# First expert's rows picked by a matmul with a selection matrix, a pair of experts moved ahead of additions, and the last tile's scattered rows added on TensorE

## The chip, the cores and the metric

The kernel runs on one core of a Trainium2 chip. The metric is the device time of one execution in microseconds (us); the table below has the runs of the kernel before.

## What is computed

Two transformer blocks run over 512 tokens of 1,024 channels. The change touches only the end of the second one, a mixture of 32 experts. Each token picks one of four groups of experts by a router's logits and then two experts in the group:

```
def _hierarchical_moe(xt, w_rg, b_rg, w_re, b_re, w_gate, w_up, w_down):
    ...
    y = jnp.zeros_like(xt)
    for e in range(N_EXPERTS):
        he = jax.nn.silu(xt @ w_gate[e]) * (xt @ w_up[e])
        y = y + combine[:, e:e + 1] * (he @ w_down[e])
    return y
```

`xt` is the normed row h2 of a token, `combine` its weight for the expert (zero for all but two). The result is added to x, and a last RMS norm with the vector `final_norm` gives the output. All is float32. Each expert has 3 MB of weights: gate and up of 1024x256, down of 256x1024.

## The kernel before, in words

**Routing (second_out, route_tile).** The 512 tokens stand in `xk` as four tiles of 128. For each tile t the kernel makes x (matmuls `pfo`), the logits (`plg`), the one-hot choice of both experts (`both`), and by matmuls with triangles of ones the rank of each token within its expert (`prank`). Each tile then adds to `ppos`, a table of which token stands in which slot of which expert. `pcnt` (sort_experts, line 1648) adds `both` over the four tiles, which gives the tokens of each expert. The normed rows go to DRAM as `h2d`, written by ScalarE with the channels regrouped (line 1509: it reads every eighth channel). The order in which the tiles take their steps on TensorE is written by hand in `SO`; the parts after `yield` in `tile` and `route_tile` are one step each, and the last entry of SO[1] is tile 3's last step, its two `ppos` matmuls.

**Tables.** `tables_of` turns `ppos` into token numbers (`tok`). The first three experts (AH = 3) are taken as they stand. The other 29 are sorted by their number of tokens: `cnt` (copied from `pcnt`), `key`, `rank`, and `order`, a chain on VectorE. SyncE reads `order` (line 1965) before it can issue the weight loads of any sorted expert, because it names the expert in DRAM.

**Experts (moe).** `gather(e)` fetches an expert's rows of h2d by an indirect DMA from GpSimd, `turn(e)` transposes them on TensorE and scales them by the norm's weights (`exT`), `gu(e)` multiplies by gate and up (`pgu`), `pair` or `scatter` by down. Experts with over 64 tokens scatter their rows to a buffer `yd` in DRAM; smaller ones go in pairs or fours: `ex_few` multiplies (`pyf`, float32), `ex_parts` scales the product on ScalarE and, as a remainder, on VectorE (`ys`), and `ex_add` brings the rows to their tokens by a matmul with a selection matrix (`psel`), after which VectorE adds PSUM to xk (line 1921). A selection is used for four tiles, two additions each; `waiting` holds the additions not yet done.

**Weights and PSUM.** Weight loads go through SyncE's queue in program order into rings of buffers: gate and up five experts ahead, down three ahead. Experts 0 to 2 and their weights are loaded before the routing ends. In this part `pb` hands out three PSUM banks in turn (tag A), `po` one (tag O); every fourth `psel` takes the one of `po`.

**End (finish).** Tiles 0 to 3 in turn: the scattered rows of tiles 2 and 3 are read back (`back`, two loads of 512 KB each into `yb`) and added by VectorE (`back_add`, line 2055), then the last four experts' rows are added. ScalarE squares each tile; one reciprocal root for all four (`rsq`, ten short VectorE instructions) and four scalings `fo` by VectorE (line 1941) follow, each with its output DMA. On TensorE the last part is in the order of the code (manual_schedule); elsewhere a scheduler places the instructions.

Of the kernel before, what the change touches and what calls it, by code (L numbers as in the profile page):

```python
# [24 lines left out]
NE = 32  # L25
# [5 lines left out]
PTC = 2  # L31
PS2 = (3, 2, 2)
FT = ((0, 4, 3),)
HB = 2


# [76 lines left out]
class K:  # L113
# [1344 lines left out]
    def second_out(self):  # L1458

        nc, I, sp = self.nc, self.I, self.sp  # L1460
        xk, yT, xp = self.xk, self.yT, self.xp
        self.ring.append(self.pool("experts1", side="right"))
        self.ep = self.pool("experts", side="right")
        rp = self.rp = self.pool("route", side="right")
        c = self.pool("out2")
        self.wsl = self.ep.tile([128, 32 + NX], F32, name="wsl")
        self.scat = self.ep.tile([128, 32 + NX], U32, name="scat")
        self.tok = self.ep.tile([128, 32 + NX], U32, name="tok")
        self.exinfo = self.ep.tile([1, 1 + NX], I32, name="exinfo")
        self.order = self.ep.tile([1, NE - AH], I32, name="order")  # L1470
        self.h2d = self.dr.tile([512, 1024], F32, name="h2d")
        wo = I["w_out_2"][0].rearrange("(k p) n -> p k n", p=128)
        us = [[self.wunit(wo[:, 4 + 2 * j:6 + 2 * j, c0:c0 + 512], [128, 2, 512]) for j in range(2)] for c0 in (0, 512)]
        wr, br = self.wr, self.br

        self.fwc = self.ep.tile([128, 8], F32, name="fwc")
        nc.gpsimd.dma_start(self.fwc, I["ffn_norm_2"][0].rearrange("(p k) -> p k", k=8))
        self.xgs = [rp.tile([128, 1024], F32, name="xg0")]
        nc.gpsimd.memset(self.xgs[0], 0.0)
        R = self.R = self.route_setup(rp)  # L1480

        def tile(t):

            x = xk[:, t, :]
            ss = sp.tile([128, 2], F32, name="h2s", bufs=2)
            for i, c0 in enumerate((0, 512)):
                p = self.pt("pfo") if i else self.pc("pfo")
                for k in range(4):
                    self.mm3(p, [y[:, 4 + k, t * 128:(t + 1) * 128] for y in yT], [x[:, k % 2, :] for x in us[i][k // 2]],
                             k == 0, k == 3)  # L1490
                o = xk[:, t, c0:c0 + 512]
                nc.vector.scalar_tensor_tensor(o, p, self.rsh[1][:, t:t + 1], o, op0=OP.mult, op1=OP.add)
                junk = self.op.tile([128, 512], F32, name="oT", tag="oT", bufs=2)
                nc.scalar.activation(junk, o, AF.Square, accum_out=ss[:, i:i + 1])
                yield
            rs = sp.tile([128, 1], F32, name="h2r", bufs=2)
            h = c.tile([128, 1024], F32, name="h2", tag="h2", bufs=2)
            y = c.tile([128, 8, 128], F32, name="x2T", tag="x2T", bufs=2)
            nc.vector.tensor_tensor(ss[:, 0:1], ss[:, 0:1], ss[:, 1:2], op=OP.add)
            self.turn8(y, x)  # L1500
            self.rsq(rs, ss[:, 0:1], 1.0 / D, EPS)
            yield
            pl = self.pt("plg")[:, :36]
            for k in range(8):
                nc.tensor.matmul(pl, y[:, k, :], wr[:, k, :], start=(k == 0), stop=(k == 7))
            nc.vector.scalar_tensor_tensor(R["lg"][:, t], pl, rs, br, op0=OP.mult, op1=OP.add)

            h3 = h.rearrange("p (k c) -> p k c", k=8)
            nc.scalar.activation(h3, x.rearrange("p (c k) -> p k c", k=8), AF.Copy, scale=rs)
            nc.scalar.dma_start(self.h2d[t * 128:(t + 1) * 128, :], h)  # L1510
            yield from self.route_tile(t, R, rp)

        tiles = [tile(t) for t in range(4)]
        for t in SO[0]:
            next(tiles[t], None)
        with self.tc.manual_schedule(engines={mybir.EngineType.PE}):
            for t in SO[1]:
                next(tiles[t], None)
        self.route_end()
        c.release()  # L1520
        self.op.release()


    def route_setup(self, c):
        nc = self.nc
        V = nc.vector
        R = {}
        io = R["io"] = c.tile([128, 128], F32, name="io")
        nc.gpsimd.iota(io, pattern=[[1, 128]], base=0, channel_multiplier=0, allow_small_or_imprecise_dtypes=True)
        R["rev"] = c.tile([128, 32], F32, name="rev")  # L1530
        V.tensor_scalar(R["rev"], io[:, :32], -1.0, 32.0, op0=OP.mult, op1=OP.add)
        jp = c.tile([128, 128], F32, name="jp2")
        nc.gpsimd.iota(jp, pattern=[[1, 128]], base=0, channel_multiplier=-1, allow_small_or_imprecise_dtypes=True)
        R["before"] = c.tile([128, 128], F32R, name="before")
        V.tensor_scalar(R["before"], jp, 0.0, None, op0=OP.is_gt)
        R["one"] = c.tile([128, 128], F32R, name="one2")
        V.tensor_scalar(R["one"], jp, -1000.0, None, op0=OP.is_ge)
        R["val"] = c.tile([128, 4, 2], F32, name="val")
        nc.gpsimd.iota(R["val"], pattern=[[128, 4], [512, 2]], base=-2048, channel_multiplier=1,
                       allow_small_or_imprecise_dtypes=True)  # L1540
        R["oh"] = c.tile([128, 4, 2, 32], F32, name="roh")
        R["both"] = c.tile([128, 4, 32], F32R, name="both")
        R["lg"] = c.tile([128, 4, 36], F32, name="lg")
        R["max"] = c.tile([128, 3, 4], F32, name="rmax")
        R["ps"] = c.tile([128, 4, 2], F32, name="rps")
        R["w"] = c.tile([128, 4, 2], F32, name="rw")
        R["pos"] = self.po("ppos")[:, :32]
        return R

    def route_tile(self, t, R, c):  # L1550
        nc = self.nc
        V = nc.vector
        rev = R["rev"]
# [22 lines left out]
        k, km = first(rest, m1, 32, "f1")  # L1576
        V.tensor_scalar(oh[:, 1], k, km, None, op0=OP.is_equal)
        V.tensor_tensor(both[:, t], oh[:, 0], oh[:, 1], op=OP.add)
        yield

        pr = self.pt("prank")[:, :64]
        for u in range(t):
            nc.tensor.matmul(pr[:, 0:32], R["one"], both[:, u], start=(u == 0), stop=False)
        nc.tensor.matmul(pr[:, 0:32], R["before"], both[:, t], start=(t == 0), stop=True)
        for k in range(2):
            x = new(32, "rx")
            V.tensor_tensor_reduce(x, pr[:, 0:32], oh[:, k], 1.0, 0.0, OP.mult, OP.add, R["ps"][:, t, k:k + 1])
# [322 lines left out]

        self.nc.vector.tensor_scalar(sel, self.io512, f, None, op0=OP.is_equal)

    def ex_add(self, sel, parts, n, t):

        for c in (slice(0, 512), slice(512, 1024)):
            self.nsel = getattr(self, "nsel", -1) + 1
            p = self.po("psel") if self.nsel % 4 == 3 else self.pb("psel")
            for k in range(2):
                self.nc.tensor.matmul(p, sel[:n, t * 128:(t + 1) * 128], parts[k][:n, c], start=(k == 0), stop=(k == 1))
            x = self.xk[:, t, c]  # L1920
            self.nc.vector.tensor_tensor(x, p, x, op=OP.add)

    def finish(self, add):

        nc = self.nc
        raw = self.eraw
        fs = raw("fs")[:, :8].rearrange("p (a t) -> p a t", a=2)
        os = []
        for t in range(4):
            add(t)  # L1930
            x = self.xk[:, t, :]
            o = raw("fo")
            nc.scalar.activation(o, x, AF.Square, accum_out=fs[:, 0, t:t + 1])
            os.append(o)
            for a, b, at in FT:
                if at != t:
                    continue
                self.rsq(fs[:, 1, a:b], fs[:, 0, a:b], 1.0 / D, EPS)
                for u in range(a, b):
                    o, rs = os[u], fs[:, 1, u:u + 1]  # L1940
                    nc.vector.scalar_tensor_tensor(o, self.xk[:, u, :], rs, self.fin, op0=OP.mult, op1=OP.mult)  # L1941
                    nc.sync.dma_start(self.out[0, u * 128:(u + 1) * 128, :], o)

    def moe(self):
# [37 lines left out]
            if e < NE:  # L1982
                X[e] = self.ex_turn(xgs[e % 2], mp, cap[e], e < 2)

        gather(0)
        gather(1)
        turn(0)
        gather(2)
        self.io512 = mp.tile([128, 512], F32, name="io512")
        nc.gpsimd.iota(self.io512, pattern=[[1, 512]], base=0, channel_multiplier=0, allow_small_or_imprecise_dtypes=True)  # L1990
# [79 lines left out]
        def step(e):  # L2070
# [22 lines left out]
            if full and e + 1 < NE:  # L2093
                waiting.extend(full + (t,) for t in range(4))

        for e in range(3):
            step(e)
        with tc.manual_schedule(engines={mybir.EngineType.PE}):
            for e in range(3, END):
                step(e)  # L2100
            load(END)
            for t in (2, 3):
                back(t)
            for e in range(END + 1, NE):
                gu(e)
                turn(e + 1)
                add(1)
                fold(e)
            add(4)
            pair(NE - 3)  # L2110
            full = pair(NE - 1)

        def last(t):
            if t > 1:
                back_add(t)
            self.ex_add(*full, t)

        self.finish(last)
        self.overflow(mp, xgs[0])
# [73 lines left out]
```

## Time and profile before

| | us |
|---|---|
| median of 3 runs | 1417.26 |
| lowest, highest | 1412.39, 1419.44 |
| profiled execution, time | 1414.1 |
| profiled execution, span | 1412.3 |
| TensorE busy | 1289.8 (91%) |
| VectorE busy | 939.0 (66%) |
| ScalarE busy | 611.6 (43%) |

The profile is of one execution; times in it count from the start of its span. The experts take about the last 300 us: from 1111 us on the 16 DMA engines move weights nearly without a pause until 1378 us, and the rest up to 1412.3 is the last additions, the norm and the output. Names such as `pgu` are the program's tiles. A float32 matmul shows as two records with two weight loads, so 64 records are 32 matmuls.

### The profile page before, as it was taken

Reading aid. Unit: us, or ns where it says so; the run is one execution under the profiler, and the core shown is the slowest. Engines: PE = TensorE matmul, PEld = TensorE weight load, DVE = VectorE, ACT = ScalarE, POOL = GpSimd, SP = SyncE. Lnnn points to the kernel's source line nnn. Section 1 sums busy time; section 2 is a strip of 40 time slices with the busy share of each in tenths; the row PEclk is TensorE's granted clock in tenths of the full one; section 3 lists DMA queues with packets and bytes.
Section 4 is the critical chain, followed back from the end, with each engine's and each line's share of the span. In section 5 each row is a group of like instructions: output and inputs, shape, how many; then the busy total and the mean of one; then the engine's idle time right before and its main releaser. Section 6 shows DMA issues by size and latency. Waiting matters only on the chain. (4 is left out here: it accounts for less than half of the span.)

```text
span 1412.3 us, 22313 instructions
## 1 busy us (share of the span) xinstructions
PE 1289.8 (91%) x7958; PEld 1021.3 (72%) x7958; DVE 939.0 (66%) x2062; ACT 611.6 (43%) x1197; POOL 312.4 (22%) x412
## 2 busy tenths in 40 slices
PE   4999999999989999899999999999999799998792
PEld 2888778877868788677877778787788776674350
DVE  5789998566643689998776463676766733534565
ACT  4553155445641474256574153777655211111122
POOL 5333032322220234133222020211110111111100
PEclk9999999999999999999998999999999799999996
DMA  9643355435132254416143356333333799999992
GB/s 342 161 129 108 102 147 159 132 99 182 60 135 61 91 127 150 139 46 166 39 124 109 140 173 172 96 82 128 97 127 118 255 389 387 369 373 375 391 401 91
DMA packets 166772, 246.18 MB, mean 174 GB/s; under 512 B 46788, under 2 KB 102810, under 8 KB 166660
## 3 DMA queue, kind: packets, MB, share of 16 engines
q1 hardware_dynamic: 161116, 234.95, 50.1%
q0 software_dynamic: 4864, 7.66, 2.0%
q10 hardware_dynamic: 680, 2.13, 0.4%
q8 instruction: 64, 1.05, 0.3%
q14 instruction: 48, 0.39, 0.1%
HBM read 220.69 MB, written 32.28 MB: 179 GB/s over the span
## 5 line engine op out<-in xcount | busy, mean ns | idle before, releaser
L185 DVE TENSOR_TENSOR wlo<-wraw,whi 128x1024 fp32r<-128x1024 f32 (+3 forms) x98 | 118.2, 1212 | 60.2 <-ACT whi L184 59.7
L184 ACT ACTIVATE whi<-wraw 128x1024 fp32r<-128x1024 f32 (+3 forms) x98 | 100.6, 1036 | 103.1 <-PE pout L223 42.9
L221 PE MATMUL pcm<-hTh,whi 128*128 128x256 f32 (+1 forms) x288 | 102.3, 355 | 9.2 <-DVE oa L531 4.3
L571 DVE SCALAR_TENSOR_TENSOR za<-zp,vec,za 128x783 f32<-128x783 f32 (+1 forms) x120 | 108.8, 914 | 0.5
L923 POOL TENSOR_SCALAR P<-P,ll 128x768 f32<-128x768 f32 (+1 forms) x80 | 73.7, 927 | 160.2 <-DVE ll L922 143.5
L223 PE MATMUL pcm<-hTh,wlo 128*128 128x256 f32 (+1 forms) x288 | 98.4, 342 | 0.1
L222 PE MATMUL pcm<-hTl,whi 128*128 128x256 f32 (+1 forms) x288 | 97.9, 340 | 0.0
L185 DVE TENSOR_TENSOR PTl<-pPT,PTh 128x512 fp32r<-128x512 f32 x104 | 70.3, 684 | 25.2 <-ACT PTh L184 24.7
L921 ACT ACTIVATE P<-pS,nm 128x768 f32<-128x768 f32 (+1 forms) x80 | 65.0, 816 | 36.6 <-DVE nm L919 30.4
L184 ACT ACTIVATE PTh<-pPT 128x512 fp32r<-128x512 f32 x104 | 60.7, 597 | 45.8 <-PE pPT L936 41.5
L1814 POOL DMA_INDIRECT xg<-h2d,tok x32 | 31.5, 986 | 214.2 <-PE pturn L1798 159.8
L1418 POOL TENSOR_SCALAR P<-P,l 128x384 f32<-128x384 f32 (+1 forms) x64 | 33.3, 536 | 184.6 <-DVE l L1417 167.5
L919 DVE TENSOR_REDUCE nm<-pS 128x1 f32<-128x768 f32 (+1 forms) x80 | 66.0, 843 | 9.6 <-PE pS L223 8.8
L221 PEld LDWEIGHTS pcm<-hTh,whi 128*128 128x128 f32 x288 | 54.8, 190 | 17.3 <-DVE oa L531 4.9
L221 PE MATMUL pcm<-hT0h,whi 128*128 128x512 f32 x144 | 59.5, 413 | 7.7 <-DVE oa L531 5.8
L936 PE MATMUL pPT<-ident,P 128*128 128x128 f32 x416 | 63.1, 280 | 1.0 <-DVE PTl L185 0.4
L968 POOL TENSOR_TENSOR oa<-oa,ot 64x256 f32<-64x256 f32 x40 | 37.4, 935 | 99.7 <-DVE ot L967 96.3
L223 PEld LDWEIGHTS pcm<-hTh,wlo 128*128 128x128 f32 x288 | 54.7, 190 | 6.5 <-DVE wlo L185 0.6
L222 PEld LDWEIGHTS pcm<-hTl,whi 128*128 128x128 f32 x288 | 54.9, 191 | 5.1 <-issue 0.5
L222 PE MATMUL pcm<-hT0l,whi 128*128 128x512 f32 x144 | 58.4, 406 | 0.0
L223 PE MATMUL pcm<-hT0h,wlo 128*128 128x512 f32 x144 | 58.4, 406 | 0.0
L221 PE MATMUL pS<-khi,qhi 96*128 96x256 f32 (+1 forms) x144 | 51.1, 355 | 4.3 <-ACT P L921 2.4
(521 smaller groups left out, 3633.0 us busy)
## 6 DMA issues: line engine op xcount, KB each, us to landing
wraw<-in_w_in_dram SPq DMA_DIRECT2D x56, 512.0 KB, 4.8
eraw<-in_w_expert_gate_dram SPq DMA_DIRECT2D x52, 512.0 KB, 10.8
eraw<-in_w_expert_up_dram SPq DMA_DIRECT2D x52, 512.0 KB, 11.3
wraw<-in_w_mod_dram SPq DMA_DIRECT2D x48, 512.0 KB, 6.0
wl<-in_w_expert_down_dram SPq DMA_DIRECT2D x32, 512.0 KB, 6.4
wh<-in_w_expert_down_dram SPq DMA_DIRECT2D x32, 512.0 KB, 10.8
wraw<-in_w_out_dram SPq DMA_DIRECT2D x24, 512.0 KB, 3.8
wraw<-in_w_expert_gate_dram SPq DMA_DIRECT2D x12, 512.0 KB, 13.5
```

What stands on the lines that cost most here:

```text
L184: nc.scalar.activation(hi, src, AF.Copy)
L185: return (eng or nc.vector).tensor_tensor(lo, src, hi.bitcast(F32), op=OP.subtract)
L221: mm(out, lhs[0], rhs[0], start=start, stop=False)
L222: mm(out, lhs[0], rhs[1], start=False, stop=False)
L223: mm(out, lhs[1], rhs[0], start=False, stop=stop)
L571: nc.vector.scalar_tensor_tensor(a[:, :nz], z[:, k:k + nz], cfw[:, i, k:k + 1], a[:, :nz], op0=OP.mult, op1=OP.add)
L919: nc.vector.tensor_reduce(nm, S, axis=AX.X, op=OP.max, negate=True)
L921: nc.scalar.activation(P, S, AF.Exp, bias=nm, accum_out=l)
L923: nc.gpsimd.tensor_scalar(P, P, l, 0.5, op0=OP.mult, op1=OP.mult)
L936: nc.tensor.transpose(p[:, jj, i * 128:(i + 1) * 128], Ps[i][:, (j + jj) * 128:(j + jj + 1) * 128], self.ident)
L968: nc.gpsimd.tensor_tensor(o, o, t, op=OP.mult)
L1418: nc.gpsimd.tensor_scalar(Ps[i], Ps[i], l[:, i:i + 1], 1.0, op0=OP.mult, op1=OP.mult)
```

## The change

The first expert's rows are no longer gathered from DRAM. Each tile builds `sel0`, a 128x128 matrix that holds a token's norm factor in the column of its slot if the token chose expert 0 (three more VectorE instructions in route_tile: a product, a copy of the rank, and the matrix). `rows(0)` and `rows(1)` multiply it with xk, 16 float32 matmuls each, reading every eighth channel of xk as the stationary operand; the result `px0` is already transposed, and ScalarE scales it into X[0] (eight instructions, as for a gathered expert). At the end the pair of experts 28 and 29 is multiplied ahead of the last four `ex_add` of the set before, tile 3's scattered rows are read back before tile 2's and added by float32 matmuls with the identity into PSUM (`plast`), and tile 0's last scaling is split: VectorE multiplies by `final_norm`, ScalarE by the reciprocal root.

```
+        sel0 = c.tile([128, 4, 128], F32, name="sel0")
+        def rows(i):
+            p = self.x0[i].rearrange("p (k n) -> p k n", k=4)
+            for k in range(4):
+                for t in range(4):
+                    nc.tensor.matmul(p[:, k], xk[:, t, :].rearrange("p (c k) -> p k c", k=8)[:, 4 * i + k, :], sel0[:, t],
+                                     start=(t == 0), stop=(t == 3))
...
         with self.tc.manual_schedule(engines={mybir.EngineType.PE}):
-            for t in SO[1]:
+            for t in SO[1][:-1]:
                 next(tiles[t], None)
+            self.x0 = self.ph("px0")
+            rows(0)
+            next(tiles[3], None)
+            rows(1)
         self.route_end()
...
         V.tensor_tensor(both[:, t], oh[:, 0], oh[:, 1], op=OP.add)
+        f = R["first"][:, :, t:t + 1]
+        V.tensor_tensor(f[:, 0], both[:, t, 0:1].bitcast(F32), rs, op=OP.mult)
         yield
...
         nc.tensor.matmul(pr[:, 0:32], R["before"], both[:, t], start=(t == 0), stop=True)
+
+        V.tensor_copy(f[:, 1], pr[:, 0:1])
+        V.tensor_scalar(sel, R["io"], f[:, 1], f[:, 0], op0=OP.is_equal, op1=OP.mult)
...
+    def ex_add(self, sel, parts, n, t, begun=None):
+        for i, c in enumerate((slice(0, 512), slice(512, 1024))):
+            if begun:
+                p = begun[i]
+            else:
+                self.nsel = getattr(self, "nsel", -1) + 1
+                p = self.po("psel") if self.nsel % 4 == 3 else self.pb("psel")
...
+                for u in FA0:
+                    nc.vector.tensor_tensor(os[u], self.xk[:, u, :], self.fin, op=OP.mult)
                 self.rsq(fs[:, 1, a:b], fs[:, 0, a:b], 1.0 / D, EPS)
...
+                    if u in FA0:
+                        nc.scalar.activation(o, o, AF.Copy, scale=rs)
+                    else:
+                        nc.vector.scalar_tensor_tensor(o, self.xk[:, u, :], rs, self.fin, op0=OP.mult, op1=OP.mult)
...
-        gather(0)
         gather(1)
-        turn(0)
+        X[0] = mp.tile([128, 8, 128], F32, name="exT", tag="exT", bufs=2)
+        for k in range(8):
+            nc.scalar.activation(X[0][:, k], self.x0[k // 4][:, k % 4 * 128:k % 4 * 128 + 128], AF.Copy,
+                                 scale=self.fwc[:, k:k + 1])
         gather(2)
...
+        def plast(i):
+            for k in range(2):
+                nc.tensor.matmul(pl[i], self.ident, B[3, k][:, i * 512:i * 512 + 512], start=(k == 0), stop=False)
...
-            for t in (2, 3):
+            for t in (3, 2):
                 back(t)
...
+            pair(NE - 3)
             add(4)
-            pair(NE - 3)
             full = pair(NE - 1)
+            pl = [self.pt("plast") for _ in range(2)]
+            plast(0)
         def last(t):
-            if t > 1:
+            if t == 3:
+                plast(1)
+            if t == 2:
                 back_add(t)
-            self.ex_add(*full, t)
+            self.ex_add(*full, t, pl if t == 3 else None)
```

FA0 is (0,). With `begun`, ex_add adds onto the PSUM tiles that `plast` began.

On TensorE, the end of the routing stood so before (`ppos`: slot table, `pcnt`: count of each expert's tokens; x3 stands for three matmuls):

```order
L1584 MATMUL prank<-both,before 128x32
L1592 MATMUL ppos<-roh,oo 128x32 x2
L1648 MATMUL pcnt<-both,one_10893 128x32
L1592 MATMUL ppos<-roh,oo 128x32 x2
L1798 MATMUL pturn<-ident,xg_10883 128x128 x8
L1831 MATMUL pgu<-exT,eraw 128x128 x32
```

and so in the changed kernel (`px` is px0, the product's two PSUM tiles):

```order
L1602 MATMUL prank<-both,before 128x32
L1613 MATMUL ppos<-roh,oo 128x32 x2
L1490 MATMUL px_11351<-sel_10904,xk 128x128 x16
L1613 MATMUL ppos<-roh,oo 128x32 x2
L1490 MATMUL px_11352<-sel_10904,xk 128x128 x16
L1669 MATMUL pcnt<-both,one_10893 128x32
L1852 MATMUL pgu<-exT,eraw 128x128 x32
```

The last count matmul moved from between the two last pairs of `ppos` to behind all 32 new matmuls, and tile 3's `ppos` to behind 16 of them.

On TensorE, the last pairs of experts before (`pfold` is the last expert's turn back, `pyf` the down products, `psel` the selections):

```order
L1852 MATMUL pfold<-ident,eg 128x128 x4
L1919 MATMUL psel<-ys,sel 128x512 x8
L1892 MATMUL pyf<-wh,eh 32x512 x4
L1892 MATMUL pyf<-wl,eh 32x512 x4
L1892 MATMUL pyf<-wh,eh 32x512 x4
L1892 MATMUL pyf<-wl,eh 32x512 x4
L1919 MATMUL psel<-ys,sel 128x512 x16
```

and in the changed kernel:

```order
L1873 MATMUL pfold<-ident,eg 128x128 x4
L1913 MATMUL pyf<-wh,eh 32x512 x4
L1913 MATMUL pyf<-wl,eh 32x512 x4
L1943 MATMUL psel<-ys,sel 128x512 x8
L1913 MATMUL pyf<-wh,eh 32x512 x4
L1913 MATMUL pyf<-wl,eh 32x512 x4
L1943 MATMUL psel<-ys,sel 128x512 x2
L2130 MATMUL plast<-yb,ident 128x512
L1943 MATMUL psel<-ys,sel 128x512 x3
L2130 MATMUL plast<-yb,ident 128x512
L1943 MATMUL psel<-ys,sel 128x512 x7
L2130 MATMUL plast<-yb,ident 128x512 x2
```

Eight selections now stand between the two pairs of experts, and the identity matmuls between the last selections.

On VectorE, the last instructions ahead of the reciprocal root (`rv` is its first one) were:

```order
L1901 SCALAR_TENSOR_TENSOR ys<-pyf,by,ys 64x512 x4
L1921 TENSOR_TENSOR xk<-psel,xk 128x512 x4
L2055 TENSOR_TENSOR xk<-xk,yb 128x1024 x4
L1921 TENSOR_TENSOR xk<-psel,xk 128x512 x4
L233 TENSOR_SCALAR rv<-fs 128x4
```

and are in the changed kernel:

```order
L1922 SCALAR_TENSOR_TENSOR ys<-pyf,by,ys 64x512 x2
L1946 TENSOR_TENSOR xk<-psel,xk 128x512 x4
L2087 TENSOR_TENSOR xk<-xk,yb 128x1024
L1964 TENSOR_TENSOR fo<-xk,fin 128x1024
L2087 TENSOR_TENSOR xk<-xk,yb 128x1024
L1946 TENSOR_TENSOR xk<-plast,xk 128x512
L1946 TENSOR_TENSOR xk<-psel,xk 128x512 x2
L1946 TENSOR_TENSOR xk<-plast,xk 128x512
L234 TENSOR_SCALAR rv<-fs 128x4
```

Two of the four whole-tile additions are gone, the product with `final_norm` stands between the other two, and tile 3's first half is added before tile 2's.

## Rows read from the trace of the kernel before

**Rows 1.** Stretches of 50 us: length; PE, PEld, DVE, ACT, POOL; clock, DMA, GB/s.
```profile
1150.00:1200.00 50.00, 48.49 (x393) 32.44 (x386) 15.90 (x32) 8.90 (x17) 7.87 (x8) 1.00 1.02 383
...
1300.00:1350.00 50.00, 36.59 (x272) 18.58 (x274) 24.37 (x42) 7.61 (x15) 4.63 (x5) 0.90 1.02 392
```

**Rows 2.** Waits of TensorE, 1300 to 1380: total us, times, longest.
```profile
PE pyf L1892 <- DMA wh<-in_w_expert_down_dram: 12.2, 3, 6.0
```

**Rows 3.** Waits of SyncE's queue, 1110 to 1380: total us, times, longest.
```profile
SPq L1965 <- DVE order L1667: 19.6, 1, 19.6
```

**Rows 4.** Timeline of VectorE, 1101 to 1112: start, duration (us), engine, line, instruction.
```profile
1101.33 0.33 DVE L1591 TENSOR_SCALAR oo<-io,rps,val 128x128 f32<-128x128 f32 x1
...
1105.79 0.18 DVE L1650 COPY cnt<-pcnt 128x32 f32<-128x32 f32 x1
...
1111.96 0.16 DVE L1667 CAST order<-order 1x29 int32<-1x29 f32 x1
```

**Rows 5.** Timeline of SyncE's queue, 1110 to the end.
```profile
1113.50 0.94 SPq L1770 DMA_DIRECT2D eraw<-in_w_expert_gate_dram  x2
...
1369.59 4.16 SPq L2051 DMA_DIRECT2D yb<-yd  x4
1397.35 3.92 SPq L1942 DMA_DIRECT2D out_dram<-fo  x4
```

**Rows 6.** Timeline of TensorE, 1103 to 1135, with the idle time before in brackets.
```profile
1103.37 1.04 PE L1592 MATMUL ppos<-roh,oo 128*128 128x32 f32 x4
1104.22 0.37 PE L1648 MATMUL pcnt<-both,one 128*128 128x32 f32 x1
...
1111.73 1.94 PE L1798 MATMUL pturn<-ident,xg 128*128 128x128 f32 x8 [6.25 <-DMA xg<-h2d,tok]
1113.46 7.81 PE L1831 MATMUL pgu<-exT,eraw 128*128 128x128 f32 x64
...
1123.69 7.39 PE L1831 MATMUL pgu<-exT,eraw 128*128 128x128 f32 x64
```

**Rows 7.** Timeline of VectorE, 1380 to 1401.
```profile
1381.85 1.53 DVE L1901 SCALAR_TENSOR_TENSOR ys<-pyf,by,ys 64x512 fp32r<-64x512 f32 x2 [0.19 <-ACT ys L1899]
1383.42 2.48 DVE L1921 TENSOR_TENSOR xk<-psel,xk 128x512 f32<-128x512 f32 x4
1385.82 4.62 DVE L2055 TENSOR_TENSOR xk<-xk,yb 128x1024 f32<-128x1024 f32 x4
1390.36 2.48 DVE L1921 TENSOR_TENSOR xk<-psel,xk 128x512 f32<-128x512 f32 x4
1394.05 0.17 DVE L233 TENSOR_SCALAR rv<-fs 128x4 f32<-128x4 f32 x1 [1.21 <-ACTq L2131]
...
1396.04 4.87 DVE L1941 SCALAR_TENSOR_TENSOR fo<-xk,fs,fin 128x1024 f32<-128x1024 f32 x4
```

**Rows 8.** Timeline of ScalarE, at 1099 and from 1380 to 1394.
```profile
1099.04 2.17 ACT L1509 ACTIVATE h<-xk,h2r 128x1024 f32<-128x1024 f32 x1 [3.79 <-DVE h2r L242]
...
1380.43 1.39 ACT L1899 ACTIVATE ys<-pyf,by 64x512 fp32r<-64x512 f32 x2 [0.31 <-PE pyf L1892]
...
1392.87 1.06 ACT L1933 ACTIVATE fo<-xk 128x1024 f32<-128x1024 f32 x1
```

**Rows 9.** One stretch of 1 us: PE busy, granted clock, DMA share, GB/s.
```profile
1104.00:1105.00 1.00, 1.00 (x6) 0.50 0.00 0
```

**Rows 10.** Timeline of TensorE, 1130 to 1381, a down product and the last pairs.
```profile
1130.91 1.02 PE L1871 MATMUL pye<-wh,eh 128*128 128x512 f32 x2
1131.78 1.02 PE L1871 MATMUL pye<-wl,eh 128*128 128x512 f32 x2
...
1374.67 2.12 PE L1919 MATMUL psel<-ys,sel 128*128 128x512 f32 x8
1376.72 1.06 PE L1892 MATMUL pyf<-wh,eh 128*32 128x512 f32 x8
...
1379.32 1.04 PE L1892 MATMUL pyf<-wl,eh 128*32 128x512 f32 x8
```

More of the change, by code (lines that the diff above doesn't have):

```diff
@@ L33 @@
 FT = ((0, 4, 3),)
+FA0 = (0,)
 HB = 2
@@ L1510, in tile @@
             nc.scalar.dma_start(self.h2d[t * 128:(t + 1) * 128, :], h)
-            yield from self.route_tile(t, R, rp)
+            yield from self.route_tile(t, R, rp, rs, sel0[:, t])
         tiles = [tile(t) for t in range(4)]
@@ L1531, in route_setup @@
         V.tensor_scalar(R["rev"], io[:, :32], -1.0, 32.0, op0=OP.mult, op1=OP.add)
-        jp = c.tile([128, 128], F32, name="jp2")
+        R["oh"] = c.tile([128, 4, 2, 32], F32, name="roh")
+        jp = R["oh"].rearrange("p a b c -> p (a b c)")[:, :128]
         nc.gpsimd.iota(jp, pattern=[[1, 128]], base=0, channel_multiplier=-1, allow_small_or_imprecise_dtypes=True)
@@ L1540, in route_setup @@
                        allow_small_or_imprecise_dtypes=True)
-        R["oh"] = c.tile([128, 4, 2, 32], F32, name="roh")
         R["both"] = c.tile([128, 4, 32], F32R, name="both")
@@ L1546, in route_setup, with route_tile @@
         R["w"] = c.tile([128, 4, 2], F32, name="rw")
+        R["first"] = c.tile([128, 2, 4], F32, name="rfirst")
         R["pos"] = self.po("ppos")[:, :32]
         return R
-    def route_tile(self, t, R, c):
+    def route_tile(self, t, R, c, rs, sel):
         nc = self.nc
@@ L1911, in ex_select @@
         self.nc.vector.tensor_scalar(sel, self.io512, f, None, op0=OP.is_equal)
[L1913 to L1917, printed above, removed]
+    def ex_add(self, sel, parts, n, t, begun=None):
[5 more added lines that the diff above has]
+                p = self.po("psel") if self.nsel % 4 == 3 else self.pb("psel")
             for k in range(2):
-                self.nc.tensor.matmul(p, sel[:n, t * 128:(t + 1) * 128], parts[k][:n, c], start=(k == 0), stop=(k == 1))
+                self.nc.tensor.matmul(p, sel[:n, t * 128:(t + 1) * 128], parts[k][:n, c], start=(k == 0 and not begun),
+                                      stop=(k == 1))
             x = self.xk[:, t, c]
@@ L1940, in finish @@
                     o, rs = os[u], fs[:, 1, u:u + 1]
-                    nc.vector.scalar_tensor_tensor(o, self.xk[:, u, :], rs, self.fin, op0=OP.mult, op1=OP.mult)
+                    if u in FA0:
+                        nc.scalar.activation(o, o, AF.Copy, scale=rs)
+                    else:
+                        nc.vector.scalar_tensor_tensor(o, self.xk[:, u, :], rs, self.fin, op0=OP.mult, op1=OP.mult)
                     nc.sync.dma_start(self.out[0, u * 128:(u + 1) * 128, :], o)
```

## The prediction, made before the changed kernel ran

> **What bounds the kernel now.** The change sits at both ends of the expert stage, so I read the stretches of that stage first. Between 1150 and 1200 the sixteen DMA engines are busy all the time (share 1.02, 383 GB/s), and so they are between 1300 and 1350, where TensorE is busy only 36.6 of 50 us [rows 1]. Nearly all of those bytes are expert weights. Early in the stage TensorE is almost full too (48.5 of 50), but then it catches up with the weights: from 1300 on it waits 12.2 us for down weights [rows 2]. So the stream of weights sets the pace, and its length cannot shrink, since every expert's 3 MB is read either way. What can move is its start. SyncE's queue stood still for 19.6 us until VectorE had written `order` [rows 3]; that ended at 1112.1 [rows 4], and the first load of a sorted expert went out at 1113.50 [rows 5], 1.4 us later. The chain behind it: the last `pcnt` on TensorE at 1104.22 [rows 6], the copy `cnt` at 1105.79, then 6.3 us of VectorE instructions to the cast of `order` [rows 4]. The gather of expert 0 runs beside that chain: TensorE waits 6.25 us for it [rows 6], but that is a wait of an engine with a queue of weights already loaded, not of the stream.
>
> After the stream the end is serial: the last down product, ScalarE's and VectorE's parts of it, additions, the root, four scalings, the output DMA. VectorE is nearly without a pause from 1381.85 to 1400.9 [rows 7].
>
> **The selection product.** It removes one gather, TensorE's eight transposes (1.94 us at the low clock) and the 6.25 us wait [rows 6]. It adds 32 float32 matmuls of 128x128, and ScalarE's eight scalings stay. A gate-and-up product is the same 32 matmuls: 7.39 us, 0.231 us each, at a granted clock of 1.00 [rows 6]. That would be the price if reading every eighth channel cost TensorE nothing. The one instruction of the trace that reads the same tile at the same stride is ScalarE's: 2.17 us for 128x1024, where the contiguous read of it takes 1.06 [rows 8], a ratio of 2.05. At that ratio a matmul is 0.473 us and the 32 are 15.1 us. [...] One row is of the same engine, the other of the same operand, and neither is nearer; I take the middle, 0.35 us each, 11.2 us, and keep 7.4 and 15.1 as ends.
>
> When does it begin? Before, tile 2's `ppos` ended at 1104.4 [rows 6]; three more VectorE instructions in each tile (the largest like `oo`, 0.33 us [rows 4]) stand in the dense chain that leads there. Most fall into gaps; I add 0.4 us (0 to 0.9). So it runs from 1104.8, and with tile 3's `ppos` between its halves (0.5 to 1.04 us, I take 0.8 [rows 6]) it ends at 1116.8. Expert 0's gate and up product then starts about 3 us later than the old 1113.46. That costs nothing yet: TensorE has weights for three experts. The next gathers are hidden likewise: expert 1's is needed only after that product.
>
> **The count behind it.** The last `pcnt` now stands behind the whole product on TensorE, which runs its matmuls in program order. So `cnt` is copied at about 1116.8 plus 0.6 for the matmul and the hand-over, 1117.4 instead of 1105.79: 11.6 us later. Nothing else in the chain to SyncE's first load changes, so `order` and the first sorted load come 11.6 us later too, and queued behind that load on SyncE are all the other weights of 29 experts. Nothing covers this: the DMA engines have no other large work then. One credit: expert 2's gather, 128 rows of 4 KB, ran in the first moments of the stream and will now be done before it; 0.52 MB at 383 GB/s [rows 1] is 1.4 us. Net: the stream ends 10.2 us later. Its ends: 7.4 us of product with the small terms at their least and 2 us of credit for TensorE being less in SyncE's way gives 3.4; 15.1 us with no credit 16.2.
>
> [...]
>
> **The pair moved ahead.** Before, `psel` x8 took 2.12 us and the two pairs' `pyf` followed without a gap, ending at 1380.36 [rows 10]. Now the first pair's `pyf` comes first, takes a bank of `pb`, and the third of the eight `psel` tiles comes round to the same bank (three banks, the fourth and eighth selection of a set use `po`). It must wait until VectorE has read the first pair's product. That is: `pyf` 1.8 us from 1374.7 (half of the 3.64 of both pairs), ScalarE 1.39 [rows 8], VectorE behind two additions 1.53 [rows 7], so to 1379.8; then four `psel` matmuls and the second pair (0.5 and 1.8 us): 1382.1 instead of 1380.36. Price 1.8 us, since VectorE's remaining work hangs on the second pair's ScalarE part as before (1380.43 to 1381.82, then 1381.85 [rows 7, 8]). If the weights of the last pair came later than that anyway it would be 0; before, nothing waited for them.
>
> **Tile 3's rows and the split scaling.** Four additions of 1.155 us become two [rows 7]: minus 2.31. But the product with `final_norm` stands between them, not in the 1.21 us in which VectorE waits for ScalarE's last square: plus 1.16. The identity matmuls cost 0.87 us each (one float32 matmul of 512 columns, from the starts of two in [rows 10]); the second stands ahead of tile 1's selections, so VectorE's third addition waits about 0.7. And tile 3's first half is added before tile 2's, so ScalarE's square of tile 2 (1.06 and a short read of its sum) starts only 0.62 us before the last addition ends and tile 3's square queues behind it: the root starts 0.6 us later. After the root, the first output is ready 0.2 us sooner (ScalarE's 1.06 for VectorE's 1.22); the others don't count, as four outputs of 0.52 MB need 5.3 us at 392 GB/s [rows 1] from the first issue, 1397.35 [rows 5], on. Sum: -2.31 + 1.16 + 0.7 + 0.6 - 0.2, or 0. With the pair the tail is 1.8 us longer (ends: -2.5 if both stalls stay away, +3).
>
> **How the numbers follow.** 10.2 + 1.8 = 12.0 us on the profiled execution's 1414.1 (its span of 1412.3 and 1.8 around it, which stay): 1426.1. The median of the runs is 3.2 above that execution, so I forecast 1417.3 + 12.0 = 1429.3. Ends: +0.9 (1418) and +19.2 (1436.5).
>
> **Rivals.** (a) *The stride is paid in full* and the product takes 15.1 us: 3.9 more, 1433. For it: ScalarE's row. Against: the weight load may have the time hidden. (b) *The stride is free*: 3.8 less, 1425.5. (c) *The delay is absorbed*, which ends as not slower. The place is the stage up to 1300: TensorE is 97% busy in the 50 us from 1150 [rows 1] and takes weights later than they land. If it is TensorE that really sets the pace there, and the DMA engines look busy because SyncE keeps them just filled, a stream that starts late catches up, and only the tail is left: 1417.3 + 1.8 = 1419. It decides the case if by 1300 TensorE's wait for weights is still the 12.2 us of [rows 2]; if it grows by the delay, (c) is dead. Against it: the DMA share of 1.02 leaves no room to catch up. (d) *Absorbed, and the tail pays*: the third `psel` doesn't wait, and the product with `final_norm` lies in VectorE's pause; the tail is then 2.5 to 4 shorter, 1413.
>
> Chances: forecast 50%, (a) 18, (b) 12, (c) 14, (d) 6. What a measurement of this kernel can tell from no change is about 0.5%, 7 us: slower is above 1424.3, faster below 1410.2. Of (b) and the forecast's low side 6% fall within 0.5%, with all of (c) and a little of (d); of (d) and what I haven't thought of 5% are faster. So slower 0.74, same 0.21, faster 0.05. The range leaves out the lowest of (c) and (d) and the highest of (a): 1418 to 1437.
>
> **What would show it.** After: first sorted load at 1122 to 1127 instead of 1113.5, `cnt` right behind `pcnt` and that behind 32 new matmuls; their total (7.4 or 15) tells (a) from (b). TensorE's waits for weights must grow by about what the load moved. In the tail, a gap of 1 to 2 us in the middle of eight `psel`, and the `final_norm` product ahead of the root's pause. The prediction is wrong if the load moves and the last weights don't, or if `pcnt` isn't what `order` waits for.

## The result, and the profile after

The changed kernel takes 1431.66 us (median of 4 runs, 1430.53 to 1433.03) against 1415.92 us; the ratio is 1.0115, with an interval of [1.0098, 1.0132]. It is slower, by 15.7 us in the medians and 16.3 by the ratio. The profiled execution took 1430.53 us (span 1428.7), 16.4 more than the one of before.

The product first. Timeline of TensorE in the changed kernel (start, duration in us, instruction):

```profile
1103.56 7.83 PE L1490 MATMUL px<-sel,xk 128*128 128x128 f32 x32
1111.23 0.53 PE L1613 MATMUL ppos<-roh,oo 128*128 128x32 f32 x4
1111.59 7.85 PE L1490 MATMUL px<-sel,xk 128*128 128x128 f32 x32
1119.20 0.26 PE L1669 MATMUL pcnt<-both,one 128*128 128x32 f32 x1
1119.31 7.39 PE L1852 MATMUL pgu<-exT,eraw 128*128 128x128 f32 x64
```

Each half of the product is 16 matmuls in 32 records. Together they take 15.7 us, 0.49 us a matmul; gu(0), behind them, has 32 matmuls of the same shape in 7.39. The last `pcnt` comes at 1119.20 instead of 1104.22 [rows 6]. Two stretches of 1 us inside the product (length; PE, PEld, DVE, ACT, POOL; clock, DMA share, GB/s), one in each half:

```profile
1105.00:1106.00 1.00, 1.00 (x6) 1.00 (x6) 0.00 (x0) 0.00 (x0) 0.00 (x0) 0.50 0.00 0
1109.00:1110.00 1.00, 1.00 (x6) 1.00 (x6) 0.00 (x0) 0.00 (x0) 0.00 (x0) 1.00 0.00 0
```

In both, TensorE and its weight load are busy all the time and the DMA engines stand still. What hangs on `pcnt`, on VectorE and then in SyncE's queue:

```profile
1119.51 0.19 DVE L1671 COPY cnt<-pcnt 128x32 f32<-128x32 f32 x1 [7.27 <-PE pcnt L1669]
...
1125.58 0.17 DVE L1688 CAST order<-order 1x29 int32<-1x29 f32 x1
```

```profile
1127.12 0.94 SPq L1791 DMA_DIRECT2D eraw<-in_w_expert_gate_dram  x2
...
1383.39 4.16 SPq L2083 DMA_DIRECT2D yb<-yd  x4
1413.41 2.91 SPq L1972 DMA_DIRECT2D out_dram<-fo  x4
```

Against [rows 4, 5] the cast is 13.6 us later, the first sorted load 13.6, the load of `yb` that stands behind the last weights 13.8, the first output 16.1. TensorE's waits for weights from 1106 to 1400 (total us, times, longest):

```profile
PE pyf L1913 <- DMA wh<-in_w_expert_down_dram: 14.4, 3, 6.5
...
PE pye L1892 <- DMA wl<-in_w_expert_down_dram: 1.1, 1, 1.1
...
PE pyf L1913 <- DMA wl<-in_w_expert_down_dram: 0.4, 1, 0.4
PE pye L1892 <- DMA wh<-in_w_expert_down_dram: 0.4, 1, 0.4
```

They sum to 16.3 us, where before it was 12.2 [rows 2], with none that ended ahead of 1300.

Profiled executions differ by several microseconds in the stages ahead of the experts, so absolute starts mislead. I therefore count from one event that every kernel has, the last of the four `both` on VectorE (the routing's choice for the last tile, the last input of the count). It lies between 1098.4 and 1105.9 in the eleven executions; in the three whose code is the same up to it, at 1102.9 (before), 1098.4 (e2_tail) and 1104.0 (e7_delay). All starts below are us after it, worked out from the timelines; the ratio is that of the runs.

| kernel | first sorted load | gu(0) | `yb` load | end of span | ratio, 95% |
|---|---|---|---|---|---|
| before | 10.6 | 10.6 | 266.7 | 309.4 | 1 |
| changed | 24.9 | 17.1 | 281.2 | 326.5 | 1.0115 [1.0098, 1.0132] |
| e1_product | 24.9 | 17.1 | 282.7 | 327.3 | 1.0083 [1.0061, 1.0105] |
| e2_tail | 10.6 | 10.5 | 266.3 | 311.8 | 1.0008 [0.9994, 1.0022] |
| e3_count_first | 25.2 | 18.7 | 282.4 | 326.5 | 1.0091 [1.0067, 1.0115] |
| e4_contig | 18.5 | 10.7 | 277.7 | 323.2 | 1.0047 [1.0030, 1.0064] |
| e6_count_sel | 11.3 | 18.8 | 273.6 | 319.4 | 1.0060 [1.0040, 1.0080] |
| e5_order_first | 9.8 | 18.4 | 273.8 | 318.6 | 1.0080 [1.0051, 1.0109] |
| e7_delay | 26.9 | 10.6 | 284.4 | 328.8 | 1.0101 [1.0071, 1.0130] |
| e8_first_contig | 11.3 | 12.8 | 269.4 | 314.4 | 1.0024 [1.0005, 1.0043] |
| e9_swapped | 11.3 | 14.7 | 269.7 | 313.9 | 1.0033 [1.0017, 1.0049] |

A thousandth is 1.4 us. From the last `both`, the changed kernel loses 14.3 us up to the first sorted load, 14.5 up to `yb`, 17.1 up to the end.

### The profile page after: what moved, and what is told of

The parts are those of the page before. It is cut to its first block, busy times and chain, and to the rows that moved or that the text cites. A ratio compares the mean times of both kernels' runs of the same rounds, so it can differ in the third digit from the quotient of the medians.

```text
span 1428.7 us, 22446 instructions
## 1 busy us (share of the span) xinstructions
PE 1311.2 (92%) x8022; PEld 1037.7 (73%) x8022; DVE 938.6 (66%) x2072; ACT 612.1 (43%) x1198; POOL 309.9 (22%) x411
## 5 line engine op out<-in xcount | busy, mean ns | idle before, releaser
L186 DVE TENSOR_TENSOR PTl<-pPT,PTh 128x512 fp32r<-128x512 f32 x104 | 70.3, 684 | 25.2 <-ACT PTh L185 24.6
## 6 DMA issues: line engine op xcount, KB each, us to landing
eraw<-in_w_expert_gate_dram SPq DMA_DIRECT2D x52, 512.0 KB, 11.3
```

Of the source, the lines that this page charges most:

```text
L186: return (eng or nc.vector).tensor_tensor(lo, src, hi.bitcast(F32), op=OP.subtract)
```

## Which part of the change costs the time

Theory: the loss is the count behind the product, and the end of the kernel adds about 1 us. Rivals: the edits of the end cost more, or gain something that the start hides. I ran each part alone. For e1_product the end was put back:

```diff
-FA0 = (0,)
+FA0 = ()
-            for t in (3, 2):
+            for t in (2, 3):
                 back(t)
...
-            pair(NE - 3)
             add(4)
+            pair(NE - 3)
             full = pair(NE - 1)
```

and `plast` is taken out again. In e2_tail these edits stand alone, with the start of the kernel before.

> The selection product alone; the end of the kernel is put back to what it was before the change. Theory: the product stands ahead of the last count matmul on TensorE, so the sorted weights start 13.6 us later than before, and that delay is carried to the end; the edits of the end cost 0.9 us by the pair of matmuls and nothing else, so this kernel takes about 1431 us (14 to 16 us over the kernel before). Rival, the edits of the end are a good part of the loss: under 1427 us. Rival, the edits of the end pay and hide a part of the product's cost: over 1434 us.

> The edits of the end alone (pair ahead of additions, last tile's rows on TensorE, one scaling on ScalarE); the start is that of the kernel before. Theory: plus 0.9 us by the pair, the rest sums to nothing, so 1416 to 1417.5 us, 0 to 1.5 us over the kernel before; the last pair's end comes 0.5 to 1 us later than 1380.4. By the prediction's own term for the pair it would be plus 1.8 us. Rival, the edits pay where the start does not disturb them: 1 to 3 us under the kernel before.

Measured: e1_product 1429.14 us, 8.6 to 14.9 us over the kernel before by its interval; e2_tail 1416.6 against 1416.94 us, between 0.9 less and 3.1 more by the interval. The product is most of the loss, and the end is near nothing. By the ratios the product alone makes 11.8 of the 16.3 us, under the 14 to 16 that I had expected, and the end alone 1.1; the 3.4 us that are left lie within the three intervals together. The end of the pairs in e2_tail, timeline of TensorE:

```profile
1371.42 1.07 PE L1893 MATMUL pyf<-wh,eh 128*32 128x512 f32 x8
1372.30 1.04 PE L1893 MATMUL pyf<-wl,eh 128*32 128x512 f32 x8
1373.27 1.21 PE L1923 MATMUL psel<-ys,sel 128*128 128x512 f32 x4
1374.80 1.20 PE L1923 MATMUL psel<-ys,sel 128*128 128x512 f32 x4 [0.32 <-DVE xk L1926]
1375.93 1.06 PE L1893 MATMUL pyf<-wh,eh 128*32 128x512 f32 x8
1376.81 1.04 PE L1893 MATMUL pyf<-wl,eh 128*32 128x512 f32 x8
```

From the start of the first product here to the end of the last it is 6.4 us. In [rows 10] the same additions and two pairs took 5.7 (1374.67 to 1380.36); with what else stands between gate and up product 31 and that end, 7.9 against 7.0. Each addition of half a tile takes two of these `psel` matmuls, so what stands between the pairs is eight matmuls, which are four selections of two `ex_add`; the section on the change calls them eight selections and four `ex_add`. The third selection (1374.80) waits 0.32 us, for an addition. It doesn't wait for VectorE to read the first pair's product, which comes after it (timeline of VectorE in e2_tail):

```profile
1374.05 1.29 DVE L1926 TENSOR_TENSOR xk<-psel,xk 128x512 f32<-128x512 f32 x2 [0.73 <-PE psel L1923]
1375.26 1.50 DVE L1902 SCALAR_TENSOR_TENSOR ys<-pyf,by,ys 64x512 fp32r<-64x512 f32 x2
```

## Why a matmul of the product takes 0.49 us

In e4_contig the only edit is the stationary operand:

```diff
-  nc.tensor.matmul(p[:, k], xk[:, t, :].rearrange("p (c k) -> p k c", k=8)[:, 4 * i + k, :], sel0[:, t],
+  nc.tensor.matmul(p[:, k], xk[:, t, (4 * i + k) * 128:(4 * i + k) * 128 + 128], sel0[:, t],
```

> The changed kernel with the product's stationary operand read as 128 neighbouring columns in place of every eighth; so the first expert's rows come out in another order of columns, and its part of the result is another. Theory, the stride of the weight load doubles each matmul: 32 matmuls take 8 to 10 us in place of 15.7 (0.231 us each at full clock, twice that in the 3 us at half clock), the count and the first sorted load come 6 to 7.5 us earlier, and the time is 1424 to 1426 us. Rival, the 0.49 us is the price of fp32 matmuls here with any layout (the start of a product behind small matmuls, or the clock): product 15 to 16 us and no change from 1431.7 us.

Its product on TensorE:

```profile
1105.56 5.46 PE L1490 MATMUL px<-sel,xk 128*128 128x128 f32 x32
...
1111.22 3.82 PE L1490 MATMUL px<-sel,xk 128*128 128x128 f32 x32
```

9.3 us in place of 15.7, as expected. The second half, at a granted clock of 1.00, takes 3.82 us, 0.239 a matmul, where every eighth channel took 7.85: a ratio of 2.05, the same as ScalarE's in [rows 8]. The first half begins at 0.50 and is longer for it:

```profile
1106.00:1107.00 1.00, 1.00 (x7) 1.00 (x7) 0.07 (x1) 0.00 (x0) 0.00 (x0) 0.50 0.00 0
...
1112.00:1113.00 1.00, 1.00 (x12) 1.00 (x11) 0.00 (x0) 0.20 (x1) 0.36 (x1) 1.00 0.00 0
```

The strided product doesn't show this: 7.83 us in the half that began at 0.50, 7.85 in the half at 1.00, and six records in each of its two stretches of 1 us, one at 0.50 and one at 1.00. So the strided read of the weights sets its rate, not the clock. The time fell to 1423.62 us, where 1424 to 1426 had been expected; the loads began 6.4 us earlier than in the changed kernel (18.5 for 24.9). The profiled execution shown is the longest of its four (1429.15), so its end in the table stands higher than its ratio.

## A late order alone

e7_delay is the kernel before with one step of the sort repeated on VectorE; TensorE's program is untouched.

```diff
-        V.tensor_tensor(m, rank[:, None, :].to_broadcast([128, n, n]), R["io"][:, :n, None].to_broadcast([128, n, n]),
-                        op=OP.is_equal)
+        for _ in range(15):
+            V.tensor_tensor(m, rank[:, None, :].to_broadcast([128, n, n]), R["io"][:, :n, None].to_broadcast([128, n, n]),
+                            op=OP.is_equal)
```

> The kernel before, with one comparison of the sort (841 elements a partition, about 1 us) done 15 times in a row on VectorE in place of once: the order comes 13.3 to 15 us later, TensorE's work and order are untouched. Theory: a late order alone costs its own size: 1430 to 1432.5 us, with the first sorted load near 1127 and TensorE's waits for down-projection weights at 16 to 20 us (12.2 before). Rival, the product's 15.7 us on TensorE is needed for the loss and a late order is half absorbed: 1421 to 1425 us.

Measured: 1428.32 against 1413.73 us, 10.0 to 18.4 us more by the interval. That is 1.7 us under the expected 1430 to 1432.5, and well above the rival's 1421 to 1425. SyncE's wait for `order`, 19.6 before [rows 3], and TensorE's largest wait for weights from 1300 on:

```profile
SPq L1966 <- DVE order L1668: 35.8, 1, 35.8
```

```profile
PE pyf L1893 <- DMA wh<-in_w_expert_down_dram: 14.5, 4, 6.8
```

The first load is 16.3 us later, counted from the last `both`; the time is 14.3 us longer by the ratio, and the end 19.4 in the profiled execution, which is the longest of its four (1434.63). So a late order costs about its size, and no work on TensorE is needed for the loss. The expected delay of 13.3 to 15 us was too short by 1.3 at its upper end, since other instructions of VectorE stand between the repeats (1.03 us each, a new one every 1.10 to 1.28 us); TensorE's waits for weights sum to 23.3 us, above the 16 to 20 expected.

## The count ahead of the product

If the order is all, it must be enough to issue the count ahead of the product:

```diff
             self.x0 = self.ph("px0")
+            next(tiles[3], None)
+            R["pcnt"] = self.pt("pcnt")[:, :32]
+            for u in range(4):
+                nc.tensor.matmul(R["pcnt"], R["one"], R["both"][:, u], start=(u == 0), stop=(u == 3))
             rows(0)
-            next(tiles[3], None)
             rows(1)
...
```

> The changed kernel with the last ppos and the four count matmuls put ahead of the product on TensorE; the work is the same. Theory, what costs is that the count waits for the product: order is there by 1111 to 1112.5, the first sorted weights are loaded at 1112.5 to 1114, gu(0) still begins near 1119, its delay of 6 us goes into TensorE's waits for weights, and the time is 1415.5 to 1418.5 us, 13 us less than the changed kernel. Rival, TensorE's added work itself costs (gu(0) 5.8 us later than before): 1421 to 1424 us even with the loads early.

Neither came: 1431.21 us, and the first load as late as in the changed kernel. VectorE shows why:

```profile
1109.46 0.19 DVE L1672 COPY cnt<-pcnt 128x32 f32<-128x32 f32 x1 [0.46 <-PE pcnt L1534]
...
1124.74 1.03 DVE L1678 TENSOR_REDUCE rank<-sx 128x29 f32<-128x841 f32 x1 [13.76 <-PE px L1490]
...
1129.58 0.16 DVE L1689 CAST order<-order 1x29 int32<-1x29 f32 x1
```

The count is there at 1109.46, early as planned. But the third step of the sort waits 13.76 us for `px`, with which it shares no data. What it shares is memory: `rank` belongs to the pool of the expert stage, which is laid out where the second output product's pool stood, and the product reads `sel0` out of that. In the changed kernel this second gate is hidden behind the first. That the memory is the cause was inferred from the pools; to test it, e6_count_sel keeps e3's order and puts `sel0` into a buffer that is free until the product is over:

```diff
-        sel0 = c.tile([128, 4, 128], F32, name="sel0")
+        sel0 = self.xgs[0][:, :512].rearrange("p (t n) -> p t n", t=4)
```

> As the run with the count first, but the selection matrix sel0 stands in the buffer of gathered rows (xg0, which the first expert no longer needs) and not in the pool that is released before the sort. There the reduction that makes rank waited 13.8 us for the product, since its tile lies where sel0 lay. Theory: with that wait gone too, the order is there about 9.7 us after the last both on VectorE (9.1 in the kernel before, 23.4 in the changed one), the first sorted weights are loaded 11 us after it, and the time is 1416.5 to 1419.5 us: 12 us less than the changed kernel, though TensorE's work and gu(0)'s start stay as in the run before. Rival, TensorE's added work sets the pace (gu(0) comes 8 us later than in the kernel before): 1423 to 1426 us with early loads.

The same step on VectorE:

```profile
1108.24 1.03 DVE L1678 TENSOR_REDUCE rank<-sx 128x29 f32<-128x841 f32 x1
```

The wait is gone, so it was the memory, and the first load goes out 11.3 us after the last `both` (10.6 before). The time is 1422.52 against 1413.73 us, 5.7 to 11.3 more than before by the interval; by the ratios that is some 8 us less than the changed kernel, but 3 us above the theory's range and next to the rival's. SyncE's queue, its first loads and one of its waits (1100 to 1300; the wait for gate and up products was 6.3 us in 4 before):

```profile
1114.40 0.94 SPq L1792 DMA_DIRECT2D eraw<-in_w_expert_gate_dram  x2
1115.53 0.86 SPq L1792 DMA_DIRECT2D eraw<-in_w_expert_up_dram  x2
1117.20 0.87 SPq L1792 DMA_DIRECT2D wraw<-in_w_expert_gate_dram  x2
1118.27 0.92 SPq L1792 DMA_DIRECT2D wraw<-in_w_expert_up_dram  x2
1124.75 1.23 SPq L1792 DMA_DIRECT2D eraw<-in_w_expert_gate_dram  x2
```

```profile
SPq L1792 <- PE pgu L1853: 19.5, 12, 4.7
```

After two experts' gate and up weights the queue stops until gu(0) gives back its buffers, and gu(0) begins at 1121.88, 18.8 us after the last `both`, 8.2 later than before. So there seems to be a third gate: the first gate and up product, late because the selection product stands ahead of it.

## Two checks of the third gate

If gu(0) holds what is left, a shorter product must give most of it back. e8_first_contig is e6 with e4's edit. e9_swapped is e6 with the operands exchanged and the rows turned as before (the added lines of e9 that differ from e6; what they replace is left out):

```diff
...
+            for t in range(4):
+                nc.tensor.matmul(self.x0[i], sel0[:, t], xk[:, t, i * 512:i * 512 + 512], start=(t == 0), stop=(t == 3))
...
+        for i in (1, 0):
+            nc.scalar.copy(xgs[0][:, i * 512:i * 512 + 512], self.x0[i])
+        turn(0)
...
```

> As e6_count_sel, with the product's stationary operand read as 128 neighbouring columns (the first expert's rows then come out in another order of columns, and its part of the result is another). In e6_count_sel the loads began early, but the third load waited for gu(0)'s buffers: SyncE waited 19.5 us for gate and up matmuls (6.3 before), because gu(0) began 18.8 us after the last both (10.6 before). Theory: what is left of the loss there is gu(0)'s lateness, that is the product's length. A product of 8 to 9.5 us puts gu(0) at 11.5 to 13.5 us after the last both, SyncE's wait falls to 6 to 10 us, and the time is 1414 to 1418 us against about 1415 of the kernel before. Rival, the rest is lost elsewhere (the later gather of the third expert's rows, the end): 1420 us or more.

> As e6_count_sel, with the operands of the product exchanged: the selection matrix is loaded as weights and the rows move, 8 matmuls of 128x512 in place of 64 records of 128x128, then two copies on ScalarE into the buffer of gathered rows and the eight turns of the kernel before. Everything is computed. The nearest rows: pye of 128x512 takes 0.43 us a record with two records to a product (2 in 1.02 with its pipeline), so 16 records take 6.9 us. Theory: product 7 us, copy 0.5 to 1 us, turns 1 to 2 us, gu(0) at 12.5 to 14.5 us after the last both (18.8 in e6_count_sel), and the time is 1415 to 1419 us, 4 to 7 us less than e6_count_sel. Rival, copies and turns eat the gain: gu(0) at 17 us or later and 1421 us or more.

In one point the text on e9 needs a correction: its rows keep the channels in their own order, where the stored rows of `h2d` are regrouped by eights, so the first expert's part of the result is another there too.

Product and gu(0) of e8, then of e9, and SyncE's wait for gate and up products in e8:

```profile
1109.05 9.58 PE L1490 MATMUL px<-xg,xk 128*128 128x128 f32 x64
1118.46 7.31 PE L1853 MATMUL pgu<-exT,eraw 128*128 128x128 f32 x64
```

```profile
1108.03 9.49 PE L1488 MATMUL px<-xk,xg 128*128 128x512 f32 x16
1118.19 1.09 PE L1817 MATMUL pturn<-ident,xg 128*128 128x128 f32 x8 [0.68 <-ACT xg L2015]
1119.31 0.49 PE L1850 MATMUL pgu<-exT,eraw 128*128 128x128 f32 x2
```

```profile
SPq L1792 <- PE pgu L1853: 9.3, 9, 3.5
```

e8: gu(0) at 12.8, SyncE's wait down from 19.5 to 9.3, the `yb` load 4.1 us earlier than in e6, and 1418.49 against 1413.86 us, 0.7 to 6.1 more than before. The time lies 0.5 us above what I had expected and the product 0.1, gu(0) and the wait within; the mechanism is as expected. e9: a product of 9.5 us, not 7, gu(0) at 14.7 and 1419.48 us, each just outside the expected bounds; the loss is 2.4 to 6.9 us. Both fit the third gate. Neither beats the gather: gu(0) begins 10.6 us after the last `both` in the kernel before, and no product with the count ahead of it gets there.

The opposite check is e5_order_first: e6 with an order that comes earlier still, while gu(0) stays late (the four count matmuls are put ahead of two `ppos`, and the sort ahead of the token table on VectorE).

> As the run before it, and the sort also stands ahead of the token table of the first three experts on VectorE, with the count ahead of two of the four last ppos matmuls; the table and its gathers come some 6 us later. Theory: the stream's start sets the end, so an order 1 to 1.5 us earlier gives back as much: 1415.5 to 1418 us. Rival, the later gathers (rows of the second expert) make TensorE wait between gu(0) and gu(1) and cost more than that: 1419 us or more.

The load went out 1.5 us earlier than in e6 (9.8 for 11.3), and nothing came of it: `yb` at 273.8 against 273.6, 1424.95 us against 1422.52, with overlapping intervals. My theory for this run fell. The rival's time came, but not by its reason: from gu(0) to gu(1) it is 9.7 us in both kernels, and TensorE waits for no gather there. SyncE's wait for gate and up products is 19.7 us, against 19.5 in e6. So with gu(0) late, an earlier order was worth nothing.

So two delays run side by side in the changed kernel. The order is 14.3 us late and gu(0) 6.5; each alone costs about its size (e7 the one, e6 the other, with 8.2 and a `yb` 6.9 us later). `yb` is 14.5 us late, so the longer of the two decides. They don't add. None of these kernels is faster than the one before.

## Why the prediction was right, step by step

The sign and the mechanism held: slower, because the count stands behind the product; and the time lies in the range. The forecast of 1429.3 lay 2.4 us under 1431.66, but part of that nearness is luck. I had added 12.0 us to a median of 1417.3, and the median in the comparison is 1415.92: the change itself took 15.7 us by the medians and 16.3 by the ratio, about 4 more than I forecast. Rival (a), 15.9 us by its terms, came nearer, and its condition is what was measured; I gave it 18%, the forecast 50%.

**The bound** was right. The stream's start sets the end; e7 shows it without any product, and rival (c) is dead. But the sign that I named for it failed: TensorE's waits for weights grew by 4.1 us, from 12.2 to 16.3, where the load moved by 14.3. By that sign alone (c) would have stayed open; what rules it out is that `yb`, behind the last weights, moved by 14.5, and e7. TensorE itself came 6.5 us later to the stream, and between gu(0) and the last gate and up product it was busy 6.3 us longer with the same work (length; PE, PEld, DVE, ACT, POOL; clock, DMA, GB/s; before, then changed):

```profile
1113.50:1371.40 257.90, 240.32 (x1929) 159.32 (x1928) 119.75 (x259) 45.55 (x95) 36.30 (x38) 0.98 1.01 380
```

```profile
1119.30:1386.70 267.40, 246.65 (x1930) 161.72 (x1929) 127.51 (x279) 45.33 (x95) 35.22 (x37) 0.96 0.98 369
```

The mean granted clock is lower there, 0.96 for 0.98; how much of the 6.3 us that makes is not worked out. So the late stream showed only in part as waits for weights.

**The product** is the mis-sized term: 15.7 us, not 11.2. Rival (a) had its price, 15.1. I took the middle between a row of the same engine and a row of the same operand; the operand's row was the right one. The granted clock, 0.50 at that place before [rows 9], was no cause: the half that began at 0.50 took 7.83 us, the half at 1.00 took 7.85.

**The count** followed as said. From the last `both`, `cnt` is copied at 17.29 us instead of 2.91 [rows 4], 14.4 later where 11.6 was predicted, and the load moved by 14.3. The 2.8 us between them are 4.5 more for the product, less three small terms: the product began 0.6 us earlier than I took it to, 0.2 us and not 0.8 lie between its halves, and `cnt` came 0.1 us after its end, not 0.6. The sentence that gu(0)'s later start costs nothing was wrong as a reason: in this kernel it is covered by the later order, and in e6 it costs.

**The credit** of 1.4 us for the gather out of the stream's way isn't seen: load and `yb` moved alike, by 14.3 and 14.5. The stream between them took 255.7 to 259.2 us in the kernels whose loads gu(0) didn't hold, so 1.4 us could hardly be read.

**A term that I didn't have**: 1.5 us between the `yb` load and the last gate and up product. The last wait for weights ends at 1354.61 in the changed kernel and at 1340.54 in the kernel before. Stretches right behind it, before and then changed:

```profile
1340.00:1345.00 5.00, 4.46 (x25) 1.75 (x26) 0.57 (x1) 1.15 (x2) 0.33 (x1) 0.68 1.02 406
1345.00:1350.00 5.00, 3.61 (x25) 2.32 (x25) 4.82 (x9) 0.30 (x2) 0.57 (x1) 1.00 1.03 405
```

```profile
1354.00:1359.00 5.00, 4.39 (x22) 1.42 (x22) 0.00 (x0) 0.68 (x1) 0.00 (x0) 0.50 1.04 413
1359.00:1364.00 5.00, 4.59 (x17) 3.09 (x17) 4.56 (x7) 0.68 (x1) 0.90 (x1) 0.61 1.01 390
```

After its wait of 6.5 us TensorE has a granted clock of 0.50 in the first of these stretches and 0.61 in the second; before, after one of 6.0, it has 0.68 and 1.00. The same instructions up to the next large gate and up product take 9.2 us there, 7.9 before, 1.3 of the 1.5. That the change causes this is not shown. In e7_delay, without a product, they take 9.3 us after a wait of 6.8, at 0.50 from 1362 to 1367 and 0.86 in the next 5 us. In e2_tail, whose loads are on time, the longest wait for weights from 1300 on is 5.8 us, and from the `yb` load to the last gate and up product it is 3.36 us (3.35 in the changed kernel, 1.82 before). In e9_swapped, with a product, that wait is 6.0 us and that time 2.17. So the time came out differently after much the same wait; what the clock was there in these last two is not shown. The kernel before has a short time there in its profiled execution, which at 1414.1 us lies under both medians of that kernel (1417.3 and 1415.92); that is also why e2_tail ends 2.4 us later in the table, where its ratio says 1.1.

**The pair** costs 0.9 us, not 1.8 (in the changed kernel as in e2). The stall of the third `psel` until VectorE has read the first pair's product doesn't exist: in e2 and in the changed kernel that `psel` begins before the read. What is paid are pauses of some tenths, the longest of 0.32 us for an addition. Which bank the third `psel` took I haven't worked out.

**Tile 3's rows and the split scaling** came to nothing, as said, and by the terms that I gave: the product with `final_norm` between the additions, a pause of 0.50 us for the third addition (0.7), the root's wait 1.66 instead of 1.21 us, on VectorE:

```profile
1401.51 1.29 DVE L1946 TENSOR_TENSOR xk<-psel,xk 128x512 f32<-128x512 f32 x2 [0.50 <-PE psel L1943]
1402.71 1.21 DVE L2087 TENSOR_TENSOR xk<-xk,yb 128x1024 f32<-128x1024 f32 x1
1403.84 1.22 DVE L1964 TENSOR_TENSOR fo<-xk,fin 128x1024 f32<-128x1024 f32 x1
...
1410.24 0.17 DVE L234 TENSOR_SCALAR rv<-fs 128x4 f32<-128x4 f32 x1 [1.66 <-ACT fo L1958]
```

From the end of the last pair to that root it is 13.66 us, before 13.69; the first output then goes out 0.1 us sooner (0.2 predicted), and from there to the end it is 0.3 longer. Sum from the last `both`: 14.5 + 1.5 + 0.9 + 0.2 = 17.1 us, in an execution whose last `both` came 0.7 us earlier: 16.4.

## What to carry to other kernels

In this kernel the start of the longest stream set the time. Look for it, and keep every instruction that feeds it ahead of work that only saves a wait elsewhere: here a wait of 6.25 us on TensorE was exchanged for 14.3 us in the start of the weights. Before you move work out of the way, look for the gates behind the first one: a pool that is laid out over the operand, and buffers that the late engine still holds. Here a strided read of the same operand, on another engine, priced the strided weight load (15.1 us for 15.7 measured), and the matmul's shape didn't (7.4).

## What the runs showed of the hardware

A float32 matmul of 128x128 whose stationary operand is read at a step of 32 bytes takes 0.49 us, with six records in 1 us at a granted clock of 0.50 as well as at 1.00; with neighbouring columns 0.239 at 1.00. And 16 records of 128x512 took as long as 64 of 128x128 with neighbouring columns (9.49 us in e9_swapped and 9.58 in e8_first_contig; the mean granted clock from 1100 to 1150 was 0.87 and 0.86).
